# A streamed decoder layer on one core: state-chain matmuls kept together, weight splits fixed among the substitution's rows, convolutions issued ahead of operand splits

## The chip, the cores and the metric

The kernel runs on one core of one Trainium2 chip. The metric is the device time of one execution in microseconds (us). Three executions of the kernel before took 1177.01, 1178.71 and 1179.49 us; the median is 1178.71 us. Engines are named as in the profile: PE multiplies matrices, DVE (vector) and ACT (scalar) do elementwise work, POOL is the third elementwise engine, SP issues most DMAs.

## The reference

One layer of a hybrid recurrent decoder runs for 512 prompt tokens and 64 sample tokens (8 sequences of 8), 576 in all. One wide projection feeds three branches, whose outputs are gated, projected and merged:

```python
xn = rmsnorm(x, g_norm)
u, za, xb, zb, q, zc, gates = split_in(xn @ w_in)
oa, s_last, shift_last = rwkv7_branch(u, za, shift0, s0, ...)   # 16 heads of 64
ob, h_last, conv_last  = rglru_branch(xb, zb, conv0, h0, ...)   # width-4 convolution, gates, scan
oc = cross_attn(q, zc, mem_k, mem_v)
merged = g_a * (oa @ w_br_a) + g_b * (ob @ w_br_b) + g_c * (oc @ w_br_c)
y = x + merged @ w_out
# rwkv7_branch, token by token, for each head:
sa = einsum("bhvk,bhk->bhv", s, -kk_t)
s  = s * w_t + sa * (kk_t * a_t) + v_t * k_t
o  = einsum("bhvk,bhk->bhv", s, r_t)
```

The kernel computes the RWKV recurrence in chunks of 64 tokens: inside a chunk a triangular 64x64 system is inverted, and between chunks the state is carried by a chain of matmuls.

## The kernel before, in words

**The stream.** All wide projections are cut into units of 128 output columns (class `Unit`, L310). `Stream.step` (L343) issues the work in small portions: one step is one block of 128 inputs, three products (high weight x high input, high x low, low x high) for two halves of 288 tokens, so 6 matmuls of 128x288; a unit has 8 steps, 48 matmuls. `st.go(n)` issues n steps, `st.until(label)` runs to the end of a unit. All these matmuls are issued in the helper `K.mm` and so have line L71 in the profile; they are called stream matmuls below. `Kern.weight` (L286) brings a unit's weights: SP's queue issues a DMA into `wraw`, ACT casts it to `whi` (L293), DVE subtracts to get `wlo` (L294). Each of the three tiles has two buffers; the next unit's load is called at the first step of the current unit (L360; at the ninth where a unit goes in two halves).

**Order.** The framework's scheduler may move instructions on an engine by its own priorities. A matmul issued by `K.mm` is held in program order while `K.pin` is true (L69 to L74); before, that is only so in `lru_phase`. All other instructions may be moved.

**RWKV.** `rwkv_phase` (L861) works in four groups of two head pairs each. For each group: `prep_b` (decay, norms `rs` by small matmuls), `prep_c` (L1022: scaled keys `BKn`, transposes `vt` and `bkt`, and the products `m`, L1049, which DVE masks into `M1`, L1055), `invert` (L1059: the diagonal blocks of `M1` go out by DMA to `d1` in two halves for each pair, L1065, and come back as `X`, L1070; then 30 rows of a substitution on DVE, two instructions each, L1075 and L1077; a transposed copy `XT`, L1081; DMAs back into `M1` and `xz`), `direct`, `bonus`, `st.go(37)`, `invert2` (L1094: matmuls `z` and `w` on 32x32 tiles, four rounds of 36 matmuls, with ACT copies between), `solved` (`U`, `W` on 64x64 tiles), then the chain.

**The chain.** `chain(os, c)` (L1182) is called for the 8 chunks. A step issues: the state product `A<-sbd,ZR` (L1187, whole array, one for each pair); DVE's `plus_state`, which adds the pair's part of it to `UV` (L1180); `st.go(2)`; `dS<-UV,BKn` (L1196, four matmuls on 128x64 tiles, two for each pair; they need the added `UV`); DVE's update of the state `sbd` (L1204); `outs`, `A<-UV,M` (L1172, four matmuls on 128x64 tiles); `st.go(4)`. The 64 sample tokens go through `sample_a` after steps 1 and 4, `sample_b` (`A8`, `zx`, 32x128 tiles) after 2 and 5, `sample_c` after 3 and 6. Matmuls with a `tile_position` use a part of the array (here 128x64, 64x64, 32x128, 32x32 and 64x128); I call them tiled, and an unbroken row of them in PE's order a tiled run. All small products share four PSUM buffers (`psb`, L76).

**After RWKV.** The kernel runs the stream until unit `zc7`, then `load_split` (L474, called at L1512) brings the attention output `ocz` back from memory in 8 blocks (`oxl`), which ACT casts to `oh` (L627) and DVE subtracts to `ol` (L628). Then comes `lru_phase` (L482): `conv(j)` (L502) issues the DMA of `xe` on ACT's queue (L505), one ACT instruction and two DVE accumulations on `cva` (L511, L513), then `xc` (L515, L517); `gates(j)` multiplies `xc` on PE into `pg`.

Of the kernel before, what the change touches and what calls it, by code (L numbers as in the profile page):

```python
# [18 lines left out]
P = 128  # L19
# [27 lines left out]
class Kern:  # L47
    def __init__(self, ctx, tc, ins, outs):
# [8 lines left out]
        self.pin = False  # L57
# [228 lines left out]
    def weight(self, w, c0, eng):  # L286

        nc = self.nc
        raw = self.wp.tile([P, KC, P], F32, tag="wraw", name="wraw")
        self.dma(raw, w[:, c0:c0 + P].rearrange("(k p) c -> p k c", p=P))  # L290
        hi = self.wp.tile([P, KC, P], F32R, tag="whi", name="whi")
        lo = self.wp.tile([P, KC, P], F32R, tag="wlo", name="wlo")
        nc.scalar.copy(hi, raw)  # L293
        eng.tensor_sub(lo, raw, hi.bitcast(F32))  # L294
        return hi, lo
# [22 lines left out]
class Stream:  # L318


    def __init__(self, K):
# [4 lines left out]
        self.done = set()  # L326

# [15 lines left out]
    def step(self):  # L343
# [11 lines left out]
        if self.k == KC * u.halves:  # L355
            self.nxt = self.pick()
            self.load(self.nxt)
# [124 lines left out]
def lru_phase(K, o2, merge, operand):  # L482
# [6 lines left out]
    with tc.tile_pool(name="lruc", bufs=1, reuse_waits="tile") as lc, tc.tile_pool(name="lru", bufs=2, reuse_waits="tile") as lp:  # L489
# [81 lines left out]
        K.pin = True  # L571
# [39 lines left out]
        K.pin = False  # L611
# [249 lines left out]
def rwkv_phase(K):  # L861
# [5 lines left out]
    with ExitStack() as es:  # L867
# [90 lines left out]
        def prep_a(o):  # L958
# [5 lines left out]
            for s in range(2):  # L964
                cs = slice(HN * s, HN * s + HN)
                for n, (dst, bias) in enumerate(((tw, K.w0h), (ta, K.a0h))):
                    pl = K.psb("lora")[:, 0:HN]
                    nc.tensor.matmul(pl, wlh[:, n, :], xw2[n][:, cs], start=True, stop=False)
                    nc.tensor.matmul(pl, wll[:, n, :], xw2[n][:, cs], start=False, stop=True)
# [15 lines left out]
        def prep_b(o):  # L985
# [4 lines left out]
            for c in range(NCH):  # L990
                nc.tensor.matmul(pr_[br:br + 64, 2 * c:2 * c + 2], o.sq[:, C * c:C * c + C], K.bones2, start=True, stop=True,
# [19 lines left out]
        def bonus(o):  # L1011
# [3 lines left out]
            for s in range(2):  # L1015
                cs = slice(HN * s, HN * s + HN)
                pb = K.psb("bon")[:, 0:HN]
                nc.tensor.matmul(pb, K.bones, hi[:, cs], start=True, stop=False)
                nc.tensor.matmul(pb, K.bones, lo[:, cs], start=False, stop=True)
                nc.vector.tensor_mul(o.bon[:, cs], pb, o.v[:, cs])  # L1020

        def prep_c(o):  # L1022
            q, BK, ZR = o.q, o.BK, o.ZR
            rv = rsv[q]
            UV = o.UV = UV2[0][:, q]
            BKn = o.BKn = rg.tile([P, NCH, P], F32, tag="BKn", name="BKn")
            for c in range(8):
# [3 lines left out]
                                 o.Ps[:, :, NS:NS + 1].unsqueeze(1).to_broadcast([P, 2, NB, NS]))  # L1031
            for c0, n in ((0, 4), (4, 4), (8, 1)):
# [10 lines left out]
            M1 = o.M1 = rg.tile([P, H2, P], F32, tag="M1", name="M1")  # L1043
            for c0, n in ((0, 4), (4, 4), (8, 1)):
                pms = [K.psb("m1") for h in range(2)]
                for c in range(c0, c0 + n):
                    for w in range(2):
                        for h in range(2):
                            nc.tensor.matmul(pms[h][64 * w:64 * w + 64, P * (c - c0):P * (c - c0) + P],  # L1049
                                             BK[64 * h:64 * h + 64, c, w, :],  # L1050
                                             ZR[64 * h:64 * h + 64, c].rearrange("p a b -> p (a b)"), start=True, stop=True,
                                             tile_position=(64 * h, 64 * w))
                for h in range(2):
                    for c in range(c0, c0 + n):
                        nc.vector.scalar_tensor_tensor(M1[:, 2 * c + h, :], pms[h][:, P * (c - c0):P * (c - c0) + P],  # L1055
                                                       rv[:, c, h:h + 1], maskq[q][c == 8],
                                                       op0=ALU.mult, op1=ALU.mult)

        def invert(prs):  # L1059

            d1 = dr.tile([NQ, 32, 32], F32, tag="d1", name="d1")
            for blk in range(2):
                for o in prs:
                    q0 = (blk * G + o.q) * H2
                    nc.sync.dma_start(d1[q0:q0 + H2].rearrange("q s t -> s q t"),  # L1065
                          o.M1[o.br + 32 * blk:o.br + 32 * blk + 32, :, o.br + 32 * blk:o.br + 32 * blk + 32])
# [3 lines left out]
            nc.sync.dma_start(X, d1)  # L1070
            tmp = rt.tile([P, N], F32, tag="sq", name="Xt")[0:NQ, 0:256]
            for s in range(1, 31):
# [4 lines left out]
                nc.vector.tensor_add(X[:, 0:s, s + 1:], X[:, 0:s, s + 1:], tv)  # L1077
            nc.vector.memset(Xf[:, 0:1024:33], 1.0)
# [15 lines left out]
        def invert2(prs):  # L1094
            for g0 in (0, 9):
                pzs = [K.psb("z1") for o in prs]
                for g in range(g0, g0 + 9):
                    for o, pz in zip(prs, pzs):
                        a, b = o.br, o.br + 32
                        nc.tensor.matmul(pz[b:b + 32, 32 * (g - g0):32 * (g - g0) + 32], o.M1[a:a + 32, g, b:b + 32],  # L1100
                                         o.xz[a:a + 32, g, :], start=True, stop=True, tile_position=(a, b))
                for o, pz in zip(prs, pzs):
                    b = o.br + 32
                    nc.scalar.copy(o.xz[b:b + 32, g0:g0 + 9, :].rearrange("p a b -> p (a b)"), pz[b:b + 32, 0:288])
                pws = [K.psb("w12") for o in prs]
                for g in range(g0, g0 + 9):
                    for o, pw in zip(prs, pws):
                        a, b = o.br, o.br + 32
                        nc.tensor.matmul(pw[a:a + 32, 32 * (g - g0):32 * (g - g0) + 32], o.xz[b:b + 32, g, :],
# [463 lines left out]
```

## Time and profile before

| what | before |
|---|---|
| median of three executions | 1178.71 us |
| the profiled execution's own time | 1175.92 us |
| its span in the trace | 1174.2 us |
| mean granted clock of PE | 0.992 |
| PE busy | 1135.5 us (97%) |
| DVE busy | 709.0 us (60%) |
| ACT busy | 521.2 us (44%) |
| POOL busy | 148.0 us (13%) |

A row of the timeline has the start in us, the time from the first start to the last end of the block, the engine, line, operation, tiles and the number of records; in square brackets stands the idle time before it and what ended it. Matmuls overlap in PE, so the distance between the starts of two blocks is what a block costs, not its length. An fp32 matmul has two records (so `x8` at `dS` is four matmuls), a stream matmul one. A row of the windows has the stretch, its length, and the busy time of PE, PE's weight loads, DVE, ACT and POOL, then the granted clock, the DMA share and GB/s.

### The profile page before, as it was taken

How to read it: one execution, taken by the hardware profiler on the slowest of the kernel's cores; microseconds unless marked ns; L12 is line 12 of the kernel's file. 1: busy time of each engine (PE TensorE's matmuls, PEld its weight loads, DVE VectorE, ACT ScalarE, POOL GpSimd, SP SyncE). 2: the span in 40 equal slices, each digit the busy share in tenths (PEclk: the TensorE clock that was granted, in tenths of full speed). 3: DMA queues.
4: the chain of work that ended last, by engine and by line, in shares of the span. 5: the costliest groups of instructions: out<-in, count | busy, mean ns of one | idle time of the engine just before them, and what ended most of it. 6: DMA issues, size and time to landing. Idle time of an engine off the chain costs nothing.

```text
span 1174.2 us, 25723 instructions
## 1 busy us (share of the span) xinstructions
PE 1135.5 (97%) x10567; PEld 1064.0 (91%) x10567; DVE 709.0 (60%) x1454; ACT 521.2 (44%) x1004; POOL 148.0 (13%) x287
## 2 busy tenths in 40 slices
PE   6999999999999999999999999999999799999997
PEld 4998988899899899998899988989989799999997
DVE  5345655245883478745686745879445669684633
ACT  5454444245523365324472244642323677622333
POOL 3010000011002210003210022100121012020032
PEclk9999999999999999999999999999999899999999
DMA  5456757632334223352223423234544846566412
GB/s 141 130 198 198 223 181 233 199 101 64 95 116 113 73 66 91 109 152 55 65 86 101 132 76 76 76 97 127 139 114 136 261 134 206 151 218 179 126 37 81
DMA packets 220622, 151.49 MB, mean 129 GB/s; under 512 B 52640, under 2 KB 196106, under 8 KB 220506
## 3 DMA queue, kind: packets, MB, share of 16 engines
q1 hardware_dynamic: 217242, 146.87, 42.7%
q10 hardware_dynamic: 3264, 2.99, 0.9%
q8 instruction: 83, 1.36, 0.5%
q14 instruction: 33, 0.27, 0.1%
HBM read 120.82 MB, written 29.01 MB: 128 GB/s over the span
## 4 chain that ended last, share of the span: by engine, by line
PE 79%; DVE 6%; DMA 5%; ACT 5%; issue 4%; SPq 0%; POOL 0%; DVEq 0%; ACTq 0%; POOLq 0%
PE u L71 13%; PE g L71 12%; PE br L71 11%; PE xb L71 4%; PE za L71 4%; PE fo L71 4%; PE q L71 4%; PE zc L71 3%; PE zb L71 3%; PE kv L71 2%; PE pg L71 1%; PE m L1049 1%; DVE wlo L294 1%; PE dS L1196 1%; PE skt L65 1%
## 5 line engine op out<-in xcount | busy, mean ns | idle before, releaser
L293 ACT CAST whi<-wraw 128x1024 fp32r<-128x1024 f32 x129 | 135.2, 1048 | 313.8 <-PE g L71 91.1
L294 DVE TENSOR_TENSOR wlo<-wraw,whi 128x1024 fp32r<-128x1024 f32 x128 | 158.1, 1235 | 117.1 <-ACT whi L293 108.1
L71 PE MATMUL u<-xh,whi 128*128 128x288 f32 x400 | 92.5, 306 | 0.0
L71 PE MATMUL u<-xh,wlo 128*128 128x288 f32 x400 | 89.9, 301 | 0.0
L71 PE MATMUL u<-xl,whi 128*128 128x288 f32 x400 | 88.2, 300 | 0.0
L71 PE MATMUL g<-xh,whi 128*128 128x288 f32 x384 | 85.7, 304 | 0.0
L71 PE MATMUL g<-xl,whi 128*128 128x288 f32 x384 | 84.4, 300 | 0.0
L71 PE MATMUL g<-xh,wlo 128*128 128x288 f32 x384 | 84.1, 299 | 0.0
L71 PE MATMUL br<-oh,wlo 128*128 128x288 f32 x384 | 82.7, 297 | 1.4 <-DVE wlo L294 1.4
L71 PE MATMUL br<-oh,whi 128*128 128x288 f32 x384 | 83.6, 299 | 0.0
L71 PE MATMUL br<-ol,whi 128*128 128x288 f32 x384 | 82.3, 296 | 0.0
L71 PEld LDWEIGHTS u<-xh,whi 128*128 128x128 f32 x400 | 65.0, 188 | 6.2 <-issue 4.7
L71 PEld LDWEIGHTS u<-xh,wlo 128*128 128x128 f32 x400 | 65.1, 188 | 1.8 <-issue 0.8
L71 PEld LDWEIGHTS u<-xl,whi 128*128 128x128 f32 x400 | 64.6, 189 | 0.6 <-issue 0.2
L71 PEld LDWEIGHTS g<-xh,whi 128*128 128x128 f32 x384 | 62.4, 190 | 1.5 <-issue 1.0
L71 PEld LDWEIGHTS br<-oh,wlo 128*128 128x128 f32 x384 | 61.8, 189 | 1.9 <-DVE wlo L294 1.8
L71 PEld LDWEIGHTS g<-xh,wlo 128*128 128x128 f32 x384 | 62.4, 189 | 1.2 <-issue 1.2
L71 PEld LDWEIGHTS g<-xl,whi 128*128 128x128 f32 x384 | 62.4, 189 | 1.1 <-issue 1.0
L71 PEld LDWEIGHTS br<-oh,whi 128*128 128x128 f32 x384 | 62.2, 189 | 0.6
L71 PEld LDWEIGHTS br<-ol,whi 128*128 128x128 f32 x384 | 61.9, 189 | 0.0
L1075 DVE TENSOR_TENSOR Xt<-X 72x30 f32<-72x30 f32 (+14 forms) x120 | 39.3, 327 | 12.9 <-DMA X<-d 9.2
L71 PE MATMUL fo<-woh,oh 128*128 128x256 f32 (+1 forms) x160 | 44.9, 280 | 0.0
(392 smaller groups left out, 2856.4 us busy)
## 6 DMA issues: line engine op xcount, KB each, us to landing
wraw<-in_w_in SPq DMA_DIRECT2D x89, 512.0 KB
wraw<-in_w_mem_kv SPq DMA_DIRECT2D x16, 512.0 KB
kn<-in_cache_mem_k SPq DMA_DIRECT2D x16, 512.0 KB
kn<-in_cache_mem_v SPq DMA_DIRECT2D x16, 512.0 KB
gd<-flt SPq DMA_DIRECT2D x24, 288.0 KB
gtt<-gd SPq DMA_DIRECT2D x24, 288.0 KB
wraw<-in_w_br_c SPq DMA_DIRECT2D x8, 512.0 KB
wraw<-in_w_br_a SPq DMA_DIRECT2D x8, 512.0 KB
```

Of the source, the lines that this page charges most:

```text
L65: ins = self.nc.tensor.transpose(out, in_, self.ident[:rows, :rows])
L71: ins = self.nc.tensor.matmul(*a, **kw)
L293: nc.scalar.copy(hi, raw)
L294: eng.tensor_sub(lo, raw, hi.bitcast(F32))
L1049: nc.tensor.matmul(pms[h][64 * w:64 * w + 64, P * (c - c0):P * (c - c0) + P], BK[64 * h:64 * h + 64, c, w, :], ZR[64 * h:64 * h + 64, c].r ...
L1075: nc.vector.tensor_mul(tv, X[:, 0:s, s:s + 1].to_broadcast([NQ, s, m]), X[:, s:s + 1, s + 1:].to_broadcast([NQ, s, m]))
L1196: nc.tensor.matmul(pS[hs, C * o.q:C * o.q + C], o.BKn[:, c, hs], o.UV[:, c, hs], start=True, stop=True, tile_position=(0, 64 * h))
```

## The change

**Stream.** A flag `Kern.hold` makes DVE's weight splits keep their place in program order; while it is set, the next unit's load is called three steps later. Stream matmuls no longer go through `K.mm`; they are held in order only while the new flag `Stream.pin` is set, which only `lru_phase` does (as before, by `K.pin`).

**RWKV.** The small products (`lora`, `rs`, `bon`, `m`, `z`, `w`, `U`, `W`, `dS`, `A` and those of the samples) now go through `K.mm`, and `K.pin` is true from `bonus` to the end of the chain, so they keep their order among each other there, while the stream's matmuls stay free to move around them. `prep_c` is split: `scaled` and `products` are called right after each `prep_b`, with that pair's two `d1` DMAs; the `X` load is issued ahead of the transposes; the substitution runs after `direct` and calls `st.go(1)` after each of its 30 rows. `invert2` calls `z` for all, one step, `w` for all, three steps. The next group's units are added before the chain instead of after `solved`.

**Chain.** One step between `A` and `dS` (two before), four after (three in the last group), and the sample parts are put into two places of a chain step: those that use the whole array (`sample_a`, `sample_c`) beside `A`, the tiled ones (`sample_b`, the new `sample_o`) right behind `outs`.

**LRU.** `load_split` of `ocz` is called in four pieces of two blocks, each after a convolution, instead of all ahead of the first.

```diff
@@ Kern.weight, Stream.step
-        eng.tensor_sub(lo, raw, hi.bitcast(F32))
+        ins = eng.tensor_sub(lo, raw, hi.bitcast(F32))
+        if self.hold:
+            self.tc.keep_in_program_order(ins)
...
-        if self.k == KC * u.halves:
+        if self.nxt is None and self.k >= KC * u.halves + 3 * K.hold:
...
-                K.mm(self.ps[:, o:o + m], a[:, k, :], b[:, k, t0:t0 + m],
-                                 start=(k == 0 and q == 0), stop=(k == KC - 1 and q == 2))
+                ins = nc.tensor.matmul(self.ps[:, o:o + m], a[:, k, :], b[:, k, t0:t0 + m],
+                                       start=(k == 0 and q == 0), stop=(k == KC - 1 and q == 2))
+                if self.pin:
+                    K.tc.keep_in_program_order(ins)
@@ lru_phase
         conv(0)
+        load_c(range(0, 2))
         st.go(8)
         conv(1)
+        load_c(range(2, 4))
         st.go(6)
         gates(0)
         conv(2)
+        load_c(range(4, 6))
         st.go(5)
         gates(1)
+        load_c(range(6, 8))
@@ invert -> substitute
+            K.hold = True
             for s in range(1, 31):
...
                 nc.vector.tensor_add(X[:, 0:s, s + 1:], X[:, 0:s, s + 1:], tv)
+                st.go(1)
+            K.hold = False
@@ chain
+            full()
+            if c > 0:
+                st.go(steps[0])
             pS = K.psb("dS")
...
             outs(os, c, pA, c == 0)
...
-            st.go(4)
+            tiled()
+            st.go(steps[1])
@@ rwkv_phase, for each group
             for o in prs:
                 prep_b(o)
+                st.go(2)
+                scaled(o)
+                products(o)
                 st.go(3)
-            UV2[0] = rg.tile([P, G, NCH, P], F32, tag="UV", name="UV", bufs=1)
+            X = invert()
             for o in prs:
                 prep_c(o)
-                st.go(6)
-            invert(prs)
+                st.go(2)
             direct(prs)
+            st.go(4)
+            substitute(prs, X)
+            if g + 1 < NG:
+                st.add(*group_units(g + 1))
+            st.go(6)
+            K.pin = True
             for o in prs:
                 bonus(o)
-            st.go(37)
             invert2(prs)
...
+            fulls = {1: lambda: sample_a(o0), 4: lambda: sample_c(o0), 5: lambda: sample_a(o1)}
+            tileds = {2: lambda: sample_b(o0), 3: lambda: [sample_o(o0), sample_in(o1)],
+                      6: lambda: sample_b(o1), 7: lambda: sample_o(o1)}
+            sample_in(o0)
             for c in range(8):
-                chain(prs, c)
...
+                chain(prs, c, (1, 4) if g + 1 < NG else (1, 3), fulls.get(c, none), tileds.get(c, none))
+            K.pin = False
```

**What moves in the order.** PE, second group, a step of the chain in which a sample part (`A8`) falls, before. `u5` is a unit of the stream, `A` and `dS` are the chain's.

```order
L71 MATMUL u5_6737<-xh_78,wlo_6640 128x288
L1172 MATMUL A8_6750<-UV_5379,M1_5567 64x64 x2
L71 MATMUL u5_6737<-xh_78,wlo_6640 128x288
L1196 MATMUL dS_6791<-UV_5379,BKn_5380 64x64 x2
L71 MATMUL u5_6737<-xh_78,whi_6639 128x288
L1196 MATMUL dS_6791<-UV_5379,BKn_5527 64x64 x2
L1172 MATMUL A_6773<-UV_5379,M1_5420 64x64
L1172 MATMUL A_6773<-UV_5379,M1_5567 64x64
L1172 MATMUL A_6773<-UV_5379,M1_5420 64x64
L1172 MATMUL A_6773<-UV_5379,M1_5567 64x64
```

The step of the same group in which `A8` falls, after:

```order
L71 MATMUL A_6728<-sbd1_2645,ZR_5301 128x128
L71 MATMUL A_6728<-sbd1_2645,ZR_5436 128x128
L371 MATMUL u5_6647<-xh_78,whi_6531 128x288 x2
L371 MATMUL u5_6647<-xl_79,whi_6531 128x288 x2
L371 MATMUL u5_6647<-xh_78,wlo_6532 128x288 x2
L71 MATMUL dS_6749<-UV_5286,BKn_5332 64x64 x2
L71 MATMUL dS_6749<-UV_5286,BKn_5460 64x64 x2
L71 MATMUL A_6728<-UV_5286,M1_5342 64x64
L71 MATMUL A_6728<-UV_5286,M1_5470 64x64
L71 MATMUL A_6728<-UV_5286,M1_5342 64x64
L71 MATMUL A_6728<-UV_5286,M1_5470 64x64
L71 MATMUL A8_6762<-sbs_2646,zx_6682 32x128 x16
```

Before, the scheduler put single stream matmuls between the tiled parts, which gives three tiled runs in ten rows; after, the tiled matmuls of the step stand in one run behind six stream matmuls.

DVE, second group, the substitution's rows (`Xt` and `X`) with the split of a unit's weights (`wlo`) among them, before:

```order
L1075 TENSOR_TENSOR Xt_5681<-X_5679 72x220
L1077 TENSOR_TENSOR X_5679<-X_5679,Xt_5681 72x11x20
L1075 TENSOR_TENSOR Xt_5681<-X_5679 72x228
L294 TENSOR_TENSOR wlo_5949<-wraw_5946,whi_5948 128x1024
L1077 TENSOR_TENSOR X_5679<-X_5679,Xt_5681 72x12x19
```

The same place after:

```order
L1095 TENSOR_TENSOR Xt_5748<-X_5561 72x210
L1097 TENSOR_TENSOR X_5561<-X_5561,Xt_5748 72x10x21
L294 TENSOR_TENSOR wlo_5830<-wraw_5827,whi_5829 128x1024
L1095 TENSOR_TENSOR Xt_5748<-X_5561 72x220
L1097 TENSOR_TENSOR X_5561<-X_5561,Xt_5748 72x11x20
```

Before, splits stand behind rows 5, 12, 18 and 26, where the scheduler put them; after, they stand behind rows 10, 18 and 26 and behind the last row, and may not move.

ACT at the start of `lru_phase` (`oh` are casts of `ocz`'s blocks, `xe` the convolutions' loads, `flt` a gate), before:

```order
L627 CAST oh_11114<-oxl_11120 128x576
L505 DMA xe_11164<-xbd_73 128x603
L627 CAST oh_11114<-oxl_11124 128x576
L416 ACTIVATE flt_11230<-g15_11175 128x576
L627 CAST oh_11114<-oxl_11128 128x576
L505 DMA xe_11233<-xbd_73 128x603
L627 CAST oh_11114<-oxl_11132 128x576
L627 CAST oh_11114<-oxl_11136 128x576
L627 CAST oh_11114<-oxl_11140 128x576
L511 ACTIVATE cva_11168<-xe_11164,par_169 128x600
L627 CAST oh_11114<-oxl_11144 128x576
L511 ACTIVATE cva_11237<-xe_11233,par_169 128x600
```

And after:

```order
L636 CAST oh_11056<-oxl_11089 128x576
L510 DMA xe_11074<-xbd_73 128x603
L421 ACTIVATE flt_11148<-g14_11093 128x576
L510 DMA xe_11151<-xbd_73 128x603
L636 CAST oh_11056<-oxl_11162 128x576
L516 ACTIVATE cva_11078<-xe_11074,par_169 128x600
L636 CAST oh_11056<-oxl_11166 128x576
L516 ACTIVATE cva_11155<-xe_11151,par_169 128x600
```

Two casts fewer stand ahead of the second convolution's load, and one cast instead of five between the first load and the first `cva`.

More of the change, by code (lines that the diff above doesn't have):

```diff
@@ L1031, in prep_c, with products @@
                                  o.Ps[:, :, NS:NS + 1].unsqueeze(1).to_broadcast([P, 2, NB, NS]))
+        def products(o):
+            q, BK, ZR = o.q, o.BK, o.ZR
+            rv = rsv[q]
+            M1 = o.M1 = rg.tile([P, H2, P], F32, tag="M1", name="M1")
+            for c0, n in ((0, 4), (4, 4), (8, 1)):
+                pms = [K.psb("m1") for h in range(2)]
+                for c in range(c0, c0 + n):
+                    for w in range(2):
+                        for h in range(2):
+                            K.mm(pms[h][64 * w:64 * w + 64, P * (c - c0):P * (c - c0) + P],
+                                             BK[64 * h:64 * h + 64, c, w, :],
+                                             ZR[64 * h:64 * h + 64, c].rearrange("p a b -> p (a b)"), start=True, stop=True,
+                                             tile_position=(64 * h, 64 * w))
+                for h in range(2):
+                    for c in range(c0, c0 + n):
+                        nc.vector.scalar_tensor_tensor(M1[:, 2 * c + h, :], pms[h][:, P * (c - c0):P * (c - c0) + P],
+                                                       rv[:, c, h:h + 1], maskq[q][c == 8],
+                                                       op0=ALU.mult, op1=ALU.mult)
+            for blk in range(2):
+                q0 = (blk * G + q) * H2
+                a = o.br + 32 * blk
+                nc.sync.dma_start(d1[0][q0:q0 + H2].rearrange("q s t -> s q t"), o.M1[a:a + 32, :, a:a + 32])
+        def prep_c(o):
+            rv = rsv[o.q]
+            UV = o.UV = UV2[0][:, o.q]
+            BKn = o.BKn
             for c0, n in ((0, 4), (4, 4), (8, 1)):
@@ L1042, in prep_c, with invert @@
                                      rv[:, c0:c0 + n, :].rearrange("p c h -> p (c h)").unsqueeze(2).to_broadcast([P, 2 * n, C]))
[L1043 to L1066, printed above, removed]
+        def invert():
             X = rg.tile([P, NCH, 2, C], F32, tag="BK", name="X").rearrange("p a b c -> p (a b c)")
@@ L1094, in invert2, with half @@
         def invert2(prs):
-            for g0 in (0, 9):
+            def half(g0):
                 pzs = [K.psb("z1") for o in prs]
@@ L1113, in invert2 @@
                     nc.scalar.copy(o.M1[a:a + 32, g0:g0 + 9, b:b + 32], pw[a:a + 32, 0:288].rearrange("p (a b) -> p a b", b=32))
+            half(0)
+            half(9)
+            st.go(1)
+            above(0)
+            above(9)
+            st.go(3)
         def direct(prs):
@@ L1180, in plus_state, with chain @@
                 nc.vector.tensor_add(u, pA[o.br:o.br + 64, P * o.q:P * o.q + P], u)
-        def chain(os, c):
+        def chain(os, c, steps, full, tiled):
             cur, nxt = sbd[(c + 1) % 2], sbd[c % 2]
@@ L1310, in rwkv_phase @@
         UV2 = [None]
+        d1 = [None]
         def za_unit(p):
```

97 lines of the change are left out of this document (50 added, 47 removed).

## Prediction

> **What bounds the kernel now.** I read the page's first parts, then the chain of waits, then windows by stage.
>
> ```profile
> span 1174.2 us, 25723 instructions
> PE 1135.5 (97%) x10567; PEld 1064.0 (91%) x10567; DVE 709.0 (60%) x1454; ACT 521.2 (44%) x1004; POOL 148.0 (13%) x287
> PE   6999999999999999999999999999999799999997
> L71 PE MATMUL u<-xh,whi 128*128 128x288 f32 x400 | 92.5, 306 | 0.0
> ```
>
> PE is busy 97% of the span, with one dip in the 32nd slice (slices are 29.4 us: 910 to 940). But a record lasts 306 ns, and such records overlap, so "busy" hides gaps. The pace is in the chain of waits, in its longest stretch without a foreign instruction:
>
> ```profile
> 323.64 36.40 PE g L71 x273
> ...
> 925.31 2.97 issue
> 928.28 4.18 PE pg L71 x8
> ```
>
> 36.40 us for 273 stream matmuls is 0.1333 us each. PE sets the end; what the change can gain is time in which PE doesn't keep this pace. The windows show where that is, in the second group from `z` to the first `dS`, from there to the end of its chain, and from the end of the last chain to the LRU's first gate matmul:
>
> ```profile
> 516.70:531.00 14.30, 14.18 (x324) 13.08 (x323) 2.79 (x4) 5.77 (x13) 0.00 (x0) 1.00 0.46 130
> 531.00:583.20 52.20, 51.89 (x499) 45.90 (x498) 31.45 (x73) 21.82 (x48) 15.91 (x26) 1.00 0.25 63
> 886.60:928.30 41.70, 34.61 (x262) 34.17 (x260) 24.51 (x43) 19.36 (x32) 5.66 (x12) 0.95 0.71 226
> ```
>
> The chain's 52.20 us hold 245 stream matmuls by the order: 32.7 us at the pace, so 19.6 us go to everything else, 78 us over four groups. The third row holds 246 for group four's rest, 32.8 us, and 8.9 us of others, most of it an idle PE at a clock of 0.95. The matmuls are the same in both kernels (8807), so PE's floor doesn't move, only what lies between.
>
> **The chain.** What a tiled run costs inside the stream is read from two steps of this chain, one unsplit and one split:
>
> ```profile
> 547.15 0.45 PE L1196 MATMUL dS<-UV,BKn 128*64 128x64 f32 x8
> 547.43 0.40 PE L1172 MATMUL A<-UV,M 128*64 128x64 f32 x8
> 547.76 0.53 PE L71 MATMUL u<-xh,whi 128*128 128x288 f32 x2
> 548.13 0.43 PE L71 MATMUL u<-xl,whi 128*128 128x288 f32 x2
> ...
> 561.82 0.34 PE L1196 MATMUL dS<-UV,BKn 128*64 128x64 f32 x4
> 562.08 0.40 PE L71 MATMUL u<-xh,whi 128*128 128x288 f32 x1
> 562.42 0.34 PE L1196 MATMUL dS<-UV,BKn 128*64 128x64 f32 x4
> 562.58 0.40 PE L1172 MATMUL A<-UV,M 128*64 128x64 f32 x8
> 562.91 0.40 PE L71 MATMUL u<-xh,whi 128*128 128x288 f32 x1
> 563.15 0.43 PE L71 MATMUL u<-xl,whi 128*128 128x288 f32 x2
> ```
>
> Both hold the same four `dS`, four `A` and two stream matmuls. Unsplit they take 548.13 - 547.15 = 0.98 us, split 563.15 - 561.82 = 1.33: one more run costs 0.35. The parts: into the tiled run 0.34 against 0.24 (562.08 to 562.42 against 562.91 to 563.15), out of it 0.26 against 0.16 (561.82 to 562.08 against 562.42 to 562.58), the first stream matmul behind it 0.24 against 0.133. I take 0.30, since some of 0.35 can be a wait of the second `dS` for its `UV`. Counted in the two orders, the four chains have 65 runs before and 41 after (16, 17, 17, 15 against 11, 10, 10, 10): 24 x 0.30 = 7.2 us saved, bounds 24 x 0.25 = 6.0 and 24 x 0.35 = 8.4. Changes of tile size inside a run fall from 14 to 8; at 0.1 each, the price of entering a run, that is 0.6.
>
> [...]
>
> Waits are the second term.
>
> ```profile
> L1196 PE MATMUL dS<-UV,BKn 128*64 128x64 f32 x256 | 20.4, 242 | 2.3 <-DVE UV L1180 1.9
> L1049 PE MATMUL m<-ZR,BK 64*64 64x128 f32 x576 | 26.8, 276 | 2.6 <-DVE M L1055 2.5
> ```
>
> Only 2.3 us of true idleness stand before `dS`; delays too short to empty PE are hidden in the overlap, and distances over the pace put all of the chain's waits at about 11 us. After, `A` and `dS` are six stream matmuls (0.8 us) apart. DVE's addition for the first pair is ready about 0.74 us after the last `A` starts, for the second 1.31, so the second pair's `dS` waits some 0.15 to 0.3 in 28 steps: 4 to 8 us stay of 11. I take -2, from -5 to 0 (the wait may just fill what it had before).
>
> **The preparation.** The products `m` run pair by pair behind `prep_b`; runs from `rs` to `z` fall from 38 to 33: 5 x 0.30 = -1.5. Their waits for PSUM (2.6 above) stay: four buffers and the same DVE readers.
>
> **z and w.** Before, each round of 18 `z` is its own run for one pair, or two rounds meet:
>
> ```profile
> 516.75 0.75 PE L1100 MATMUL z<-xz,M 32*32 32x32 f32 x18
> 517.43 0.53 PE L71 MATMUL u<-xl,whi 128*128 128x288 f32 x2
> ...
> 524.33 0.67 PE L1100 MATMUL z<-xz,M 32*32 32x32 f32 x31
> 524.92 0.54 PE L71 MATMUL u<-xl,whi 128*128 128x288 f32 x2
> ```
>
> 18 records of one pair take 0.68 (0.038 each), 31 records where pairs alternate 0.59 (0.019). After, the pairs alternate throughout. Before has about half in each form; if all of 576 records in four groups fell from 0.028 on average to 0.019 it would be 5.2, but runs already mixed gain nothing. The number of runs from `z` to `dS` stays four per group. I take -2, from -4.4 to 0.
>
> **The substitution.** DVE is the engine to watch.
>
> ```profile
> 472.17 0.60 DVE L1055 SCALAR_TENSOR_TENSOR M<-m,rsv,masks 128x128 f32<-128x128 f32 x2
> 474.74 1.03 SPq L1065 DMA_DIRECT2D d<-M  x2
> 479.32 0.32 SPq L1070 DMA_DIRECT2D X<-d  x1
> 482.89 0.19 DVE L1075 TENSOR_TENSOR Xt<-X 72x30 f32<-72x30 f32 x1 [2.00 <-DMA X<-d]
> 485.45 1.23 DVE L294 TENSOR_TENSOR wlo<-wraw,whi 128x1024 fp32r<-128x1024 f32 x1 [0.17 <-ACT whi L293]
> 508.92 0.21 DVE L1077 TENSOR_TENSOR X<-X,Xt 72x30 f32<-72x30 f32 x1
> ```
>
> From 482.89 to 509.13 are 30 rows and four splits of 1.23: (26.24 - 4.9) / 30 = 0.71 us a row. A step of the stream is 6 x 0.133 = 0.80. So eight rows and a split take 6.9 us on DVE while PE uses up a unit in 6.4: DVE loses half a microsecond with each unit, some 2 us over the stage. Before, the scheduler could put a split ahead of rows; after, it is fixed behind rows 10, 18, 26 and 30. With T0 the last `m`: the masks end 0.6 later, and the DMAs there and back took from 472.77 to 482.89, so `X` lands at about T0 + 10, and the splits are ready at about 18, 26, 33 and 38. In the order of after the first of these units begins 98 stream matmuls behind T0 (13.1 us) plus 88 transposes and small matmuls (some 8 us, an estimate from their distances before), so PE needs them at about 21.4, 27.8, 34.2 and, with `z` between, 41.8. A margin of 1 to 3 us is left. `X` later by 1 to 2 us, behind another transfer on SP's queue, would cost up to 0.7 a group. I take +0.9 in all, from 0 to 2.8. The issue of `X` moves ahead of the transposes, and SP has only `wraw` and the `d1` pieces there. The cover of the four 1.2 us splits is the unit in flight; if it goes, each late microsecond is PE's.
>
> **The LRU's start.** PE waits for `pg`, which waits for `xc` of the first convolution:
>
> ```profile
> 919.45 0.34 ACTq L505 DMA_DIRECT2D xe<-xbd  x1
> 920.20 2.19 ACT L627 CAST oh<-oxl 128x576 fp32r<-128x576 f32 x3
> 922.29 0.88 ACT L511 ACTIVATE cva<-xe,par 128x600 f32<-128x600 f32 x1
> 925.13 0.88 ACT L511 ACTIVATE cva<-xe,par 128x600 f32<-128x600 f32 x1
> 924.95 0.19 POOL L506 COPY conv_st<-xe 128x3 f32<-128x3 f32 x1 [5.73 <-DMA xe<-xbd]
> 925.93 1.59 DVE L513 SCALAR_TENSOR_TENSOR cva<-xe,par,cva 128x600 f32<-128x600 f32 x2
> 927.44 0.75 DVE L515 SCALAR_TENSOR_TENSOR xc<-xe,par,cva 128x512 f32<-128x512 f32 x1
> L71 PE MATMUL pg<-xc,wbd 128*128 128x288 f32 x64 | 18.9, 443 | 6.4 <-issue 6.4
> ```
>
> In DVE's queue the first `xc` stands behind the second convolution's first accumulation (the second of the x2 at 925.93), in both kernels. That needs the second `xe`, issued at 919.45 and landed by 924.95, and its `cva`, 0.88 on ACT. Taking two casts away from in front of that issue makes it 1.4 to 2 us earlier (casts 0.68 to 0.73 each, and their waits for `oxl`); the first `cva` moves up by four casts. Then `xc` follows `xe` without the other casts: 2.6 to 4.1 of the 6.4 us go, some 0.5 comes back when the casts stand later. I take -3, from -4.5 to 0. What is late next is the same `xe` transfer, 5.5 us of it.
>
> **Sum.** -7.2 - 0.6 - 2 (chain) - 1.5 (runs in the preparation) - 2 (`z`, `w`) + 0.9 (substitution) - 3 (LRU) = -15.4. The profiled execution took 1175.92 with a span of 1174.2, and so would take 1160.5. The median of three is 2.8 above that execution, so I expect 1163.3, rounded 1163. Adding the best ends gives 8.4 + 0.6 + 5 + 1.8 + 4.4 + 4.5 = 24.7 less, 1154; the worst 6.0 + 1.2 - 2.8 = 4.4 less, 1174.
>
> **Rivals.**
>
> *Only the switch count pays.* The second `dS` pair takes the place of the old waits, `z` and `w` gain nothing, and the second `xe` is as late as before: -9.3 + 0.9 = -8.4, 1170. For it: 0.15 to 0.3 us in 28 steps is as much as was there. 0.17.
>
> *All waits go.* The best ends, 1154 or a little less. For it: the chain's DVE work (31.45 of 52.20 us) has room. Against it: the second pair's 1.31 us is over the 0.8 of six matmuls. 0.10.
>
> *Held in order, PE starves.* Mechanism: the splits fixed among the rows. It decides where `X` lands: beyond about T0 + 12, each further microsecond stands in front of four units' splits and PE waits once for it in each group. To eat up 16 us it takes 4 to 5 us a group; at 5, the sum is -16 + 20 = +4, 1182. For it: DVE loses 0.5 us a unit, and before's 10 us from masks to `X` hold 2 us in which the `d1` DMAs stood behind a `gd` on SP. Against: that was the group's worst place and is counted in T0 + 10. 0.08. [...]
>
> *The stream's matmuls move anyway.* They are not held in RWKV, so the scheduler could fill the runs again. The order shows the runs whole: 0.01.
>
> **How the numbers follow.** The forecast has 0.64 with its own range 1155 to 1168, the rivals 0.17, 0.10, 0.08 and 0.01. 1153 to 1175 takes in the first two rivals and leaves out starvation and the far end of the best case: about 0.85. About 0.2% (2.4 us) is what a measurement of this kernel can tell from no change. Faster: 0.64 + 0.17 + 0.10 less a little for a partial stall, 0.88; same 0.04; slower 0.08.
>
> **What would show it.** Right: from the first `dS` to the last chain step of groups two and three, the non-stream time falls from 19.6 to about 17 us or less; `dS` and `A` stand in one run of each step; no idleness of PE in front of a stream matmul on `wlo` in the substitution; `pg` waits 3 to 4 us, not 6.4. Wrong: rows of `g` or `xb` with idle time by DVE `wlo`; a first `X` row over 12 us behind the last `m`; `dS` with 5 us and more of idleness by DVE `UV`; a `pg` wait as before.

## The result, and the profile after

The changed kernel takes 1164.57 us (median of 11 executions, 1161.95 to 1173.64) against 1178.31 us before (11 executions, 1174.65 to 1181.71): a ratio of 0.989, 95% interval 0.9873 to 0.9907. The forecast was 1163 us. The profiled execution took 1162.3 us against 1175.92; its span is 13.6 us shorter.

The page of the changed kernel, then its windows: `z` to the first `dS` in the second group, that group's chain, and the last group's end of the chain to the first `pg`:

```profile
span 1160.6 us, 25693 instructions
PE 1118.7 (96%) x10567; PEld 1052.5 (91%) x10567; DVE 709.1 (61%) x1454; ACT 521.1 (45%) x1004; POOL 159.4 (14%) x287
```

```profile
511.69:524.11 12.42, 12.20 (x318) 11.13 (x317) 1.56 (x4) 5.84 (x15) 0.32 (x2) 1.00 0.50 132
524.11:572.98 48.87, 47.77 (x487) 43.15 (x484) 30.45 (x70) 20.35 (x46) 14.46 (x24) 1.00 0.29 74
868.05:909.41 41.36, 37.80 (x285) 37.35 (x284) 24.24 (x41) 18.18 (x32) 5.76 (x12) 1.00 0.73 214
```

A shorter stretch alone says little, since stream matmuls have moved between stages. So each stage is measured as the prediction did: its length less its stream matmuls at 0.1333 us. For the three rows these are 37, 231 and 270 matmuls, which leaves 7.5, 18.1 and 5.4 us, against 8.8, 19.6 and 8.9 before. Over the four groups (`Sf` is the transpose of the final state, the first matmul behind a chain; here the full-array 128x288 matmuls of `bon` and `lora` are taken off as well, the same number before and after):

| stage | before | after | difference | forecast |
|---|---|---|---|---|
| `rs` to `z` (products, substitution) | 77.3 | 80.6 | +3.3 | -0.6 |
| `z` to the first `dS` | 35.0 | 30.4 | -4.7 | -2 |
| first `dS` to `Sf` (the chain) | 81.8 | 73.4 | -8.4 | -9.8 |
| `Sf` to the next `rs`, three groups | 6.4 | 7.1 | +0.7 | 0 |
| last `Sf` to the first `pg` | 8.9 | 5.4 | -3.5 | -3 |
| start, and all behind `pg` | | | -1.0 | 0 |

The waits of PE that changed most, first before, then after (total, times, longest, us):

```profile
PE pg L71 <- issue: 6.4, 1, 6.4
PE m L1049 <- DVE M L1055: 2.5, 4, 0.6
PE A L1187 <- DVE sbd L1202: 0.4, 1, 0.4
```

```profile
PE m L71 <- DVE M L1056: 5.7, 7, 1.2
PE pg L71 <- issue: 3.2, 1, 3.2
PE A L71 <- DVE sbd L1236: 2.0, 3, 0.7
PE dS L71 <- DVE UV L1211: 1.7, 4, 0.6
```

The gate's wait is half of what it was, and the products' wait for DVE's masks has more than doubled. A chain step after the change, the one with `A8` in it (here `A<-sbs,zx`):

```profile
554.32 0.61 PE L71 MATMUL A<-sbd,ZR 128*128 128x128 f32 x4
554.69 0.52 PE L371 MATMUL u<-xh,whi 128*128 128x288 f32 x2
...
555.31 0.42 PE L371 MATMUL u<-xh,wlo 128*128 128x288 f32 x2
555.66 0.45 PE L71 MATMUL dS<-UV,BKn 128*64 128x64 f32 x8
555.94 0.40 PE L71 MATMUL A<-UV,M 128*64 128x64 f32 x8
556.28 1.08 PE L71 MATMUL A<-sbs,zx 128*32 128x128 f32 x32
557.29 0.54 PE L371 MATMUL u<-xh,whi 128*128 128x288 f32 x2
```

All tiled matmuls of the step stand in one run, `dS` for both pairs at once, as the order shows it.

### The profile page after: what moved, and what is told of

Same layout as the page of the kernel before. It is cut to its first block, busy times and chain, and to the rows that moved or that the text cites. A ratio compares the mean times of both kernels' runs of the same rounds, so it can differ in the third digit from the quotient of the medians.

```text
span 1160.6 us, 25693 instructions
## 1 busy us (share of the span) xinstructions
PE 1118.7 (96%) x10567; PEld 1052.5 (91%) x10567; DVE 709.1 (61%) x1454; ACT 521.1 (45%) x1004; POOL 159.4 (14%) x287
## 3 DMA queue, kind: packets, MB, share of 16 engines
q8 instruction: 83, 1.36, 0.5%
## 4 chain that ended last, share of the span: by engine, by line
PE 74%; DVE 10%; ACT 7%; DMA 5%; issue 4%; POOL 0%; SPq 0%; ACTq 0%; DVEq 0%; POOLq 0%
PE br L371 12%; PE g L371 11%; PE u L371 11%; PE q L371 4%; PE fo L71 4%; PE zc L371 4%; PE xb L371 4%; PE za L371 3%; PE zb L371 2%; PE kv L371 2%; PE A L71 2%; DVE wlo L294 2%; PE skt L65 1%; PE pg L71 1%; PE m L71 1%
## 5 line engine op out<-in xcount | busy, mean ns | idle before, releaser
L1277 POOL TENSOR_TENSOR zx<-ZR,bm 128x256 f32<-128x256 f32 x16 | 20.4, 1287 | 218.9 <-DVE X L1097 131.2
```

Source lines behind the costliest of these rows:

```text
L1277: nc.gpsimd.tensor_mul(zx[:, w], o.ZR[:, 8, w, :].rearrange("p (g t) -> p g t", g=2).unsqueeze(2).to_broadcast([P, 2, 4, 32]), K.bm4.unsqu ...
```

## The experiments

Twelve kernels, each an edit of the changed one (e3 of e2). Times are medians with the ratio to the kernel before, timed beside it; "stage" numbers are the stage time without stream matmuls, as in the table, against the changed kernel.

**e1_splits_first.** Undoes the LRU part.

```diff
+        load_c(range(0, 8))
         conv(0)
-        load_c(range(0, 2))
...
-        load_c(range(2, 4))
...
```

> The changed kernel, but the eight splits of the attention output stand ahead of the first convolution again, as before the change. Theory (the gate matmul waits for the second convolution's load, which stands behind casts on ACT's queue): the wait before pg goes from 3.2 back to about 6.4 us and the time from 1162.3 (profiled run of the changed kernel) to about 1165.8. Rival (the shorter wait came with the other arrival of the stage, not with the order on ACT): pg still waits 3 to 4 us and the time stays within 1 us of 1162.3.

1168.15 us, ratio 0.9938 (0.9913 to 0.9963); span 1164.8. Every stage from the first `rs` on is within 0.4 us of the changed kernel's, and the last one ahead of `pg` is 5.1 us longer. PE's wait in e1:

```profile
PE pg L71 <- issue: 8.3, 1, 8.3
```

The second convolution's load and its `cva`, first in the changed kernel, then in e1:

```profile
901.48 0.33 ACTq L510 DMA_DIRECT2D xe<-xbd  x1
906.88 0.89 ACT L516 ACTIVATE cva<-xe,par 128x600 f32<-128x600 f32 x1 [1.35 <-DMA xe<-xbd]
```

```profile
902.29 0.67 ACT L633 CAST oh<-oxl 128x576 fp32r<-128x576 f32 x1 [4.68 <-DMA oxl<-ocz]
903.66 0.36 ACTq L510 DMA_DIRECT2D xe<-xbd  x1
910.06 0.67 ACT L633 CAST oh<-oxl 128x576 fp32r<-128x576 f32 x1 [2.74 <-DMA oxl<-ocz]
910.64 0.88 ACT L516 ACTIVATE cva<-xe,par 128x600 f32<-128x600 f32 x1
909.92 0.19 POOL L511 COPY conv_st<-xe 128x3 f32<-128x3 f32 x1 [9.53 <-DMA xe<-xbd]
```

In e1 the load stands in ACT's queue behind a cast that waits 4.68 us for its block of `ocz`. It is issued at 903.66, and `xe` is there by 909.92, where POOL's copy of it starts. The `cva` then stands 0.7 us more behind the next cast. So the theory holds: the late issue is the larger part and the cast in front of `cva` the smaller. The wait is longer than the 6.4 us of the kernel before; why, the runs do not show.

**e2_stream_held and e3_runs_cut.** e2 holds the stream too:

```diff
-            st.go(6)
-            K.pin = True
+            K.pin = st.pin = True
+            st.go(11)
...
-            K.pin = False
+            K.pin = st.pin = False
```

with two steps behind each of the double rounds of `z` and `w`. 

> The changed kernel with the stream's matmuls also held in program order from bonus to the end of the chain, 11 steps ahead of z, 2 between z and w, 2 behind w. In the order the tiled runs of a group fall from 4 to 2 between z and dS and from 10 or 11 to 8 in the chain. Theory (a tiled run inside the stream costs about 0.30 us): 16 to 18 runs less, about 5 us faster than the changed kernel, 1157. Rival (runs cost nothing, the gain of the change was waits): no change, or some us slower because waits of z, U and dS can no longer be filled by the scheduler: 1162 to 1167.

e3 cuts each step's run in two:

```diff
+            st.go(1)
             outs(os, c, pA, c == 0)
...
-                chain(prs, c, (1, 4) if g + 1 < NG else (1, 3), ...
+                chain(prs, c, (1, 3) if g + 1 < NG else (1, 2), ...
```

> As e2_stream_held, but one of the stream's steps behind the A matmuls of a chain step is put between dS and A, so that each of the 32 chain steps has two tiled runs instead of one; the same matmuls, and dS waits as before. Theory: 32 runs x 0.30 to 0.35 us, 9.6 to 11.2 us slower than e2_stream_held, all of it in the four chains. Rival (the switch itself costs little and the chain's gain was waits): within 2 us of e2_stream_held.

e2: 1170.65 us, ratio 0.995 (0.9933 to 0.9966), slower than the changed kernel, not faster, and by more than the rival allowed. The chains did get shorter, by 2.5, 0.9 and 0.2 us in the first three groups (+0.5 in the last), which fits nine runs less. It was given back elsewhere: 3.4 us in the first group's `z` stage, where `z` waits 2.4 us and the granted clock falls behind it (0.92 over 350 to 360, 0.74 over 360 to 370); 3.6 between `rs` and `z`, with a second drop of the clock (0.83 over 450 to 460); 1.0 in each `Sf` to `rs`, where most of the 5.0 us stand that the `ot` matmuls (transposes of the result `onat`) waited for DVE instead of 0.4; and 2.3 ahead of `pg`. With the stream held, nothing filled these waits.

e3: 1174.37 us, ratio 0.9988 (0.9973 to 1.0002). That is 3.7 us over e2 in the medians and 1.0 in the profiled spans, neither the 9.6 to 11.2 of the theory nor, by the medians, the rival's 2. The chains alone grew by 7.5 us, but 2.7 came back between `rs` and `z` and 2.7 between `Sf` and `rs`, where `ot` waits 0.3 us instead of 5.0. The same step, e2 and then e3:

```profile
543.52 0.45 PE L71 MATMUL dS<-UV,BKn 128*64 128x64 f32 x8
543.81 0.57 PE L71 MATMUL A<-UV,M 128*64 128x64 f32 x11
...
545.23 0.53 PE L371 MATMUL u<-xh,whi 128*128 128x288 f32 x2
```

```profile
542.90 0.45 PE L71 MATMUL dS<-UV,BKn 128*64 128x64 f32 x8
543.28 0.53 PE L371 MATMUL u<-xh,whi 128*128 128x288 f32 x2
...
544.28 0.62 PE L71 MATMUL A<-UV,M 128*64 128x64 f32 x11
...
545.75 0.54 PE L371 MATMUL u<-xh,whi 128*128 128x288 f32 x2
```

From `dS` to the stream it is 1.71 us uncut and 2.85 cut, of which six stream matmuls are 0.80: one more run cost 0.34 here. Over whole chains the stage grew by 2.3 us in each of the first three groups, 8 runs each: 0.29 a run; waits of `dS` do not add to it, since e3 has fewer than e2 (1.2 and 2.8 us in all). In the last group it grew by 0.6 only, where e2 has a 0.7 us wait of `dS` that e3 has not. The price forecast for a run (0.30) stands inside a chain; what reaches the whole kernel also depends on which waits a longer chain covers.

**e4_pairs_apart.**

```diff
-                for g in range(g0, g0 + 9):
-                    for o, pz in zip(prs, pzs):
+                for o, pz in zip(prs, pzs):
+                    for g in range(g0, g0 + 9):
```

and the same for `w`. 

> The changed kernel with z and w issued pair by pair (nine of one pair, then nine of the other) instead of alternating pairs. Theory (the z and w matmuls of one pair follow each other at 0.038 us a record, alternating ones at 0.018 to 0.019): 144 records a group x 0.02 x 4 groups = 11 us slower than the changed kernel, all between z and dS, 1173. Rival (the gain between z and dS came from waits for ACT's copies between the rounds): within 1.5 us of 1162.3.

1169.39 us, ratio 0.9944 (0.9922 to 0.9965). The stage from `z` to `dS` grew by 1.36, 1.35, 1.21 and 1.35 us, 5.3 in all, to 8.84 in the first three groups, about the 8.75 of before. So the order of the pairs accounts for all of the 4.7 us that the change gained there, but at half of the expected size. The changed kernel's `z` first, then that of e4:

```profile
515.66 1.32 PE L71 MATMUL z<-xz,M 32*32 32x32 f32 x70
516.91 0.40 PE L371 MATMUL u<-xh,wlo 128*128 128x288 f32 x1
```

```profile
517.89 1.59 PE L71 MATMUL z<-xz,M 32*32 32x32 f32 x51
519.30 0.21 PE L71 MATMUL w<-M,xz 32*32 32x32 f32 x1
```

Alternating records follow each other at 1.25 / 70 = 0.018 us, those of one pair at 1.41 / 51 = 0.028. The step that failed is the 0.038: its 0.68 us for 18 records held both edges of a run. 144 x 0.0095 = 1.4 us a group. The e4 kernel also has one tiled run less in each of these stages, so the order of the records alone may be worth some 0.3 us more a group.

**e5_old_places.** Sample parts behind the whole step again:

```diff
-                chain(prs, c, (1, 4) ..., fulls.get(c, none), tileds.get(c, none))
+                chain(prs, c, (1, 4) ..., none, none)
+                if c in (1, 4):
+                    sample_a(prs[c // 4])
...
```

> The changed kernel with its steps (1, 4) and its held small matmuls, but the sample parts called behind a whole chain step again, as before the change. In the order the four chains have 63 tiled runs instead of 41. Theory (runs at 0.29 us, the price that cutting the runs of a held stream has shown): 22 x 0.29 = 6.4 us slower than the changed kernel, all in the chains. Rival (the gain in the chain came from holding the small matmuls in order): within 1.5 us of the changed kernel.

1179.98 us, ratio 1.0035 (1.0019 to 1.0052): the whole gain is gone, and a little more. The chains are 0.5, 5.3, 3.9 and 1.4 us longer, 11.1 in all, more than the 6.4 of the theory. `dS` waits 4.3 us for `UV` against 1.7, and in one chain the clock fell (0.83 over 540 to 550, 1.7 us lost). Without these, 6.8 us are left for 22 runs, 0.31 each. A second drop of the clock (0.73 over 610 to 620 and 0.93 over 620 to 630, 2.9 us, between `rs` and `z` of the third group) and 1.6 us behind the chains, where `za` waits for `wlo`, make up most of the rest.

**e6_products_spread.**

```diff
+                if c0 == 4:
+                    st.go(2)
...
+                K.pin = st.pin = True
                 products(o)
-                st.go(3)
+                K.pin = st.pin = False
+                st.go(1)
```

> The changed kernel with two of the stream's steps held between the second and the third set of the products m of each pair, so that DVE's masks can empty the PSUM buffers. Theory (from rs to z the changed kernel lost 3.3 us because m waits for M's masks, 5.7 us in 7 waits): the waits of m fall below 1.5 us and, with 5 runs less at 0.29, the stage gets 4 to 6 us faster: about 1157 profiled. Rival (the wait only moves, since DVE is late with the masks anyway and the X load with them): X lands later, z waits for its DMAs, and the time stays within 1.5 us.

1178.19 us, ratio 1.0018 (1.0002 to 1.0034). No wait for the masks is left, and a dearer one has come:

```profile
PE m L71 <- DVE BK L1016: 22.4, 8, 5.3
```

The first held `m` of a pair stands in PE's queue before its `BK` is made, and the stream behind it stops. The stage from `rs` to `z` is 18.4 us longer, with the clock falling four times behind or in these waits (0.66 over 290 to 300, 0.83 over 450 to 460 and over 610 to 620, 0.87 over 770 to 780); the chains are 4.7 shorter, with five runs less, and why so much was not tried. Neither expectation was right; PE starves on something held in order, as in the prediction's slower rival, but on `m` and not on the splits.

**e7_products_late.** Products behind both `prep_b` and the transposes:

```diff
             for o in prs:
                 prep_b(o)
-                st.go(2)
+                st.go(3)
+            for o in prs:
                 scaled(o)
-                products(o)
-                st.go(3)
+                prep_c(o)
+                products(o)
+                st.go(4)
             X = invert()
-            for o in prs:
-                prep_c(o)
-                st.go(2)
```

> The changed kernel with the products m behind the transposes of prep_c and behind both prep_b, as before the change, and the X load behind them. Theory (products first cost more in waits for PSUM than they save in runs): m waits 2.5 us as before instead of 5.7, but 7 more runs at 0.29 come in, so within 2 us of the changed kernel as long as z does not wait; X then lands some 3 us later against the stream, and each split of the substitution has that much less margin. Rival (products first are what keeps the substitution covered): PE waits for wlo or for the DMAs of z, 2 us and more in each group, 8 us or more slower.

1169.84 us, ratio 0.9947 (0.9929 to 0.9965). `m` waits 2.5 us for the masks, as before, but the stage from `rs` to `z` is 4.8 us longer in sum: 8 more runs by the trace (2.3 us at 0.29), and 5.0 us in which stream matmuls wait for ACT's `flt`, a wait that does not appear in the changed kernel, against 3.2 us less of waits for the masks. The chains are 2.2 us longer. No wait for `wlo` came in the substitution. Neither theory had the wait for `flt`; in this arrangement products first is worth it in spite of the masks.

**e8_old_steps.** `chain(prs, c, (2, 4), ...)` with the new places. 

> The changed kernel with the steps (2, 4) of before in the chain instead of (1, 4), the sample parts in their new places. In the order 36 runs instead of 41, and 12 instead of 6 stream matmuls between A and dS. Theory (dS of the second pair waits 0.15 to 0.3 us in each step when only six stream matmuls stand before it): 28 waits go, 4 us or more, and 5 runs at 0.29, so 5 to 6 us faster in the chains; the wait for DVE's sbd at the next A stays hidden behind four steps. Rival (these waits are already covered): only the runs, 1.5 us.

1169.87 us, ratio 0.9952 (0.9931 to 0.9972). The chains are 3.0 us shorter (1.6, 0.4, 0.3, 0.7): 1.5 by runs, and `dS` waits 0.5 us instead of 1.7. So the second pair's wait is real and about 1.5 us in all, not 4. Instead of the 5 to 6 us that the theory expected, the kernel got slower, since more is lost elsewhere: 0.7 us in each `Sf` to `rs`, where `ot` waits 3.9 us instead of 0.4, since units were used up earlier; 3.7 behind `pg`, where the branch matmuls `br` wait 2.1 us more for `whi` and `wlo` and the granted clock is lower (under 0.9 in the page's slice of 29 us there, 0.9 or more in the changed kernel's); and, in the profiled execution, a drop of the clock in the second group (0.68 over 450 to 460) that costs 3.0 us.

**e9_convs_first.** `conv(1)` directly behind `conv(0)`. 

> The changed kernel with both of the first two convolutions ahead of all splits of the attention output. Theory (what is left of the wait before pg is the second convolution's load and the casts between it and its cva): the load is issued ahead of flt and its cva follows the first cva directly, so the wait falls from 3.2 to 1.5 to 2.5 us; 1 to 1.5 us faster than the changed kernel (span 1160.6), 1159.3. Rival (the transfer itself is what lasts): no change of the wait.

1163.31 us, ratio 0.988 (0.985 to 0.991), not to be told from the changed kernel. `pg` still waits 3.0 us, not 1.5 to 2.5. ACT shows why:

```profile
902.88 0.83 ACTq L510 DMA_DIRECT2D xe<-xbd  x2
907.00 0.65 ACT L421 ACTIVATE flt<-g 128x576 f32<-128x576 f32 x1 [3.45 <-PE g L371]
909.33 0.67 ACT L636 CAST oh<-oxl 128x576 fp32r<-128x576 f32 x1 [1.68 <-DMA oxl<-ocz]
909.91 1.66 ACT L516 ACTIVATE cva<-xe,par 128x600 f32<-128x600 f32 x2
```

Both `xe` are there by 906.74 (POOL's copies of them run at 905.61 and 906.74); now the first `cva` waits in ACT's queue behind a cast that waits for `ocz`. The wait removed was replaced by the next one. In e12, with the same edit, `pg` waits 2.3 us and the stage ahead of it is 0.9 us shorter than the changed kernel's, so how much of it comes back differs.

**e10_chain_free.** The line `K.pin = True` in RWKV is left out. 

> The changed kernel without holding the small matmuls in RWKV (the pin from bonus to the end of the chain is left out); steps and places of the sample parts stay. In the order the chains have 40 tiled runs against 41, and three instead of four between z and dS of a group. Theory (the places of the sample parts make the runs, not the holding): within 1.5 us of the changed kernel, if anything 1 us faster (4 runs at 0.29). Rival (holding carries the gain of the chain): 5 us and more slower, in the chains.

1171.42 us, ratio 0.9934 (0.9903 to 0.9964); its profiled execution has two clock drops that cost 3.0 us each (0.66 over 610 to 620, 0.87 and 0.79 over 760 to 780; below). Apart from them, `z` to `dS` is 0.72 to 0.78 us longer in each group, since the scheduler then issues the first nine `z` of one pair by themselves (18 records in 0.68 us, as before the change), and the chains are 1.5 us longer, most of it in the first, where `dS` waits up to 1.4 us. Holding is worth some 4.5 us, near the rival's 5, but two thirds of it lie between `z` and `dS` and not in the chains. The count of runs shows nothing of it.

**e11_masks_ahead and e12_masks_convs.** DVE's masks are held ahead of `ta` and `BKn`'s last block; e12 has e9's edit as well.

```diff
-            nc.vector.tensor_mul(ta, o.r, o.k)
...
-                scaled(o)
                 products(o)
+                tc.keep_in_program_order(nc.vector.tensor_mul(o.ta, o.r, o.k))
+                scaled(o)
```

> The changed kernel with DVE's masks M1 held ahead of the bonus product ta and of BKn's last block, which stood before them. Theory (m waits for PSUM because DVE comes late to the masks, with ta, a split and BKn in front): the masks start 1 us earlier, the waits of m on M fall from 5.7 to 2 to 3 us, and the stage from rs to z loses 2 to 3 of its 3.3 us: span about 1158. Rival (the split of the weights is the one that holds them up): the waits stay above 4.5 us and the time within 1 us.

> Masks held ahead (as e11_masks_ahead) and both convolutions first (as e9_convs_first) together. If both theories hold the gains add, since the stages are apart: 3 to 4.5 us faster than the changed kernel, span 1156 to 1157.5, and the median below both kernels. Rival: one of them gives its gain back at the next wait, 1159 to 1161.

e11: 1163.30 us, ratio 0.9885 (0.9856 to 0.9913). The longest wait of `m` fell from 1.2 to 0.8 us, their sum only from 5.7 to 5.0, and the stage from `rs` to `z` did not get shorter, with two runs more. These are the rival's numbers, and DVE's rows fit it: a split of 1.2 us (448.69 and 463.60 in the second group) still stands in front of the masks of both pairs, and the second pair's wait rose from 0.4 to 0.8. e12: 1161.67 us (1159.46 to 1163.07, four executions), ratio 0.986 (0.9835 to 0.9885). Its median is the lowest of all, but the interval overlaps the changed kernel's, and the profiled spans (1161.3 and 1160.6) do not show a gain; that it beats the changed kernel is not shown.

## Why the prediction was right

Its sum was -15.4, the profiled executions differ by -13.6, and the mechanisms were mostly the right ones. That the sum came so close is partly luck: the products with the substitution, the chain and the stage behind it came out 3.9, 1.4 and 0.7 us worse than forecast, `z` and `w`, the LRU and the ends of the kernel 2.7, 0.5 and 1.0 better. Of the signs that it named, one run in each step, no idle time on `wlo` in the substitution and a `pg` wait of 3 to 4 us (3.2) came. The chains of groups two and three did not fall to 17 us, only to 18.1 and 18.0. Step by step:

- *A tiled run in the stream costs about 0.30 us.* Shown by e3 (0.29) and fitted by what is left of e5 (0.31). 24 runs are 7.0 us.
- *Waits of the chain, -2.* This is not shown. The chain gained 8.4 in all; less 7.0 and the forecast's 0.6 for tile sizes, which no run tested by itself, 0.8 is left. But the idle time that the profile shows in the four chains rose, from 2.6 to 4.6 us, most of it `A` on `sbd` (0.4 to 2.0). Nor is the gain spread like the runs: the first three groups gained 4.9 us with 19 runs less, the last one 3.5 with five. What gave the last group 2 us beyond its runs stays open. The prediction's doubt about the second pair's `dS` was right in kind; by e8 it costs about 1.5 us, not 4 to 8.
- *`z` and `w`, -2.* It was -4.7. The cause is alternation, as forecast (e4, 5.3 us when undone). The price per record was read too high, from rows that held the run's edges, and the share of the kernel before that already alternated was set too high as well (31 of 144 records in the rows of the second group, not half); the two errors pulled in opposite ways.
- *Products, -1.5 for five runs, and "their waits for PSUM stay".* This step failed. The waits went from 2.5 to 5.7 us, and in the first group `m` waits 0.6 us for its `BK` besides. Right behind `prep_b`, DVE still has `ta`, a split and a piece of `BKn` in front of the masks, which begin 1.9 us behind the first `m` (449.24 and 451.11). The first pair's `m` of the second group, before and then after, and DVE after:

```profile
456.50 2.88 PE L1049 MATMUL m<-ZR,BK 64*64 64x128 f32 x64
```

```profile
449.24 1.98 PE L71 MATMUL m<-ZR,BK 64*64 64x128 f32 x64
452.37 0.44 PE L71 MATMUL m<-ZR,BK 64*64 64x128 f32 x4 [1.16 <-DVE M L1056]
```

```profile
449.10 0.75 DVE L1017 TENSOR_TENSOR ta<-r,k 128x576 f32<-128x576 f32 x1
449.77 1.22 DVE L294 TENSOR_TENSOR wlo<-wraw,whi 128x1024 fp32r<-128x1024 f32 x1
450.90 0.28 DVE L1036 TENSOR_TENSOR BKn<-BK,pe 128x128 f32<-128x128 f32 x1
451.11 4.74 DVE L1056 SCALAR_TENSOR_TENSOR M<-m,rsv,mask 128x128 f32<-128x128 f32 x18
```

  The forecast looked at the buffers and the readers, and not at what is queued ahead of the readers. The stage came out at +3.3 instead of -0.6; since the substitution's +0.9 did not come either, 4.8 us are to be explained. The waits account for 3.2 and 0.6 of them, and about 1 us stays open. Part of the rise may be one of sight: the 64 records took 2.88 us before, with DVE's masks 1.65 us behind them (458.15), and 1.98 after, so some of the waiting was there before in gaps too short to be listed. And e11, which set the masks ahead of `ta`, did not shorten the stage.
- *Substitution, +0.9.* It cost nothing: no wait for `wlo` there. `X`'s first row starts 7.5 us behind the start of the last masks (468.21). The forecast's 10 was counted from there too (472.17), and not from the last `m` as it says, which starts at 470.80 before and 466.96 after. The splits end at 484.56, 492.50 and 499.65, where PE uses them at 489.21, 495.61 and 502.01. The margin shrinks from 4.6 to 3.1 to 2.4 us, so DVE does lose on PE with each of these units, as said.

```profile
475.71 0.19 DVE L1095 TENSOR_TENSOR Xt<-X 72x30 f32<-72x30 f32 x1 [0.53 <-DMA X<-d]
...
498.44 1.21 DVE L294 TENSOR_TENSOR wlo<-wraw,whi 128x1024 fp32r<-128x1024 f32 x1
```

- *Not seen: the stage `Sf` to `rs`, +0.7.* Stream matmuls of `za` wait 1.4 us for `wlo`, three times up to 0.5.
- *LRU, -3.* -3.5, by the mechanism named (e1), with a further wait behind it (e9).
- *Held in order, PE starves.* This did not decide in the changed kernel. But where the stream is held too, it stood still behind a matmul whose input came late: in e6 behind `m`, which waits 22.4 us for `BK`, and in e2 behind `z`, 2.4.
- *Not seen: the stretch behind `pg`, -1.1.* The 12 us behind the first `pg`, before and after:

```profile
928.28:940.28 12.00, 12.00 (x56) 10.44 (x57) 7.88 (x12) 8.26 (x16) 0.71 (x4) 0.76 0.52 156
```

```profile
909.41:921.41 12.00, 12.00 (x65) 10.80 (x66) 10.61 (x16) 11.30 (x21) 0.35 (x2) 0.86 0.75 228
```

  Before, the granted clock is 0.50 from 923.8 to 934.1 us, through the last 4.4 us of the wait for `pg` and 5.8 behind it; after, from 910.6 to 914.0, and this begins 1.1 us behind the wait (stream matmuls are then 0.24 us apart, at 932.74 and at 912.75). At a clock of 0.76 the 12 us lose 2.9 us, at 0.86 they lose 1.7: the difference is about the 1.1. It does not follow from the shorter wait alone: e5 with a wait of 4.0 us has a mean clock of 0.9 or more in the page's slice of 29 us there, e8 with one of 3.2 one under 0.9. So part of this gain is chance.

## What to carry to other kernels

In a stream of full-array matmuls, count the tiled runs, not the tiled matmuls: each run cost about the same here (0.29 to 0.34 us), so gather the tiled matmuls, and leave the stream itself free to fill waits. Before products are moved closer to their inputs, look at what the engine that empties their PSUM buffers has queued at that moment (here 1.9 us passed from the first `m` to the first mask, and the waits of `m` went from 2.5 to 5.7 us). A price per record is read inside a run, without its edges. What a step gains is counted over the whole kernel: in e2, e3 and e8 most of what the chains gained or lost was undone elsewhere.

## What the runs showed of the hardware

Executions of the changed kernel spread over 12 us, and the spread goes with the granted clock. e9 has the same instructions in the second group as the changed kernel, the same wait of 1.16 us, and then this:

```profile
451.88 0.43 PE L71 MATMUL m<-ZR,BK 64*64 64x128 f32 x4 [1.16 <-DVE M L1056]
...
454.01 0.68 PE L371 MATMUL g<-xh,whi 128*128 128x288 f32 x2
...
460.83 0.43 PE L371 MATMUL g<-xl,whi 128*128 128x288 f32 x2
```

From 453.6 to 460.4 a stream matmul takes 0.24 us instead of 0.133. A window of e9, then one of the changed kernel:

```profile
454.00:460.00 6.00, 6.00 (x35) 5.71 (x35) 3.89 (x11) 2.45 (x3) 0.77 (x1) 0.50 0.10 31
```

```profile
450.00:460.00 10.00, 8.84 (x112) 7.77 (x104) 9.49 (x26) 4.79 (x10) 1.59 (x1) 1.00 0.37 102
```

At 0.24 us instead of 0.133 for a stream matmul, these 6.8 us cost 3.0; e9's profiled execution had two such drops (0.68 over 450 to 460, 0.66 over 610 to 620) and took 1167.51 us, its three others 1161.15 to 1163.70. e10 had two, e8 and e5 one each, all behind a wait of `m` of 1.2 us (1.16 in e9). In the profiled executions of these four, of the changed kernel, e1, e3 and e4 that wait occurs three times each: 24 times in all, and 6 times the drop came. It is not a matter of `m` alone: in e2 and e3 the clock fell behind a wait of `z` of 1.6 and 1.7 us, in e5 behind one of `dS` of 1.9, in e6 behind or in waits of `m` for `BK` of 2.2 and more. The changed kernel's profiled execution had none in these stages; its two longest, 1170.10 and 1173.64 us, have mean clocks of 0.990 and 0.988 against 0.994 to 0.996 in the others. The drops differ in length: 6.8 us here in e9, and around `pg` 3.4 in the changed kernel and 10.2 in the one before. What sets one off the runs do not show: the same wait of 1.16 us has a drop behind it in e9 and none in the changed kernel. So in some executions more was lost behind the wait of `m` than the wait itself is long (3.0 against 1.16 us in e9). e11 and e12, whose longest wait is 0.8 us, had one execution of eight over 1164 us, the changed kernel seven of eleven; with so few, that the shorter wait prevents the drops is not shown.
